# The order of a two-layer trunk's instructions, searched for from twelve beginnings instead of one

## The chip, the cores and the metric

The kernel runs on one core of one Trainium2 chip. Its time is the device time of one execution in microseconds (us). Before the change it took 1188.26 us, the median of three runs (1187.7 to 1189.58).

## The reference

The model has two layers over 512 tokens of width 1024, in float32. Cut to what matters, a layer is:

```python
h   = rms_norm(x, g_pre_mix)
u_pool, q, k, v, iq, ik, iw = split(h @ w_in)        # 512 | 512 | 512 | 512 | 512 | 64 | 8 columns
q, k, iq, ik = rope on the first 16 of 64 columns of each head
a   = pool_mixer(u_pool)         # 4 groups of 128 channels: mean over the last 2, 4, 8 or 16 tokens
                                 # less the token itself, then a 128x128 matmul and a scale
score = sum over 8 heads of iw * relu(iq . ik / 8)   # keys of later 64-token chunks left out
b   = attention of 8 heads over the 128 keys with the highest score of each query
x   = x + rms_norm(concat(a, b) @ w_out, g_post_mix)
f   = relu(rms_norm(x, g_pre_ffn) @ w_ff1) ** 2 @ w_ff2      # width 4096
x   = x + rms_norm(f, g_post_ffn)
```

## The kernel before

**Arithmetic.** Every float32 factor is split into a high part, rounded to the matmul's format, and the remainder, and a product is three matmuls (`mm3`: high x high, high x low, low x high). The weights come from HBM through `WeightStream`: raw loads of 512 KB into two buffers (`wraw`), and two more for the MLP's first matrix (`uraw`). Each chunk of 128 rows is then split into one of eight `ws` tiles, the high part by a copy that may run on VectorE (DVE) or ScalarE (ACT), the low part by a subtraction on DVE. All but one block of the MLP's first product are done by a scheme with seven half-sized products in place of eight (`unit_products`, tiles `one` and `two`), which needs sums of weight quarters on DVE.

**Stages of a layer.** The token norm and transposes (`pre_norm`, tiles `h`, `hT`, `A`), the indexer's product and scores (`pi`, `lg`, `sc`), q, k and v (`rows_block`, tiles `pg`), meanwhile the selection of keys on DVE (`select`: 15 or 16 rounds of eight maxima and their replacement, tiles `m` and `bias`), attention for four blocks of 128 queries (`s`, `pt`, `pT`, `po`) beside the pooling mixer (`pool`, `mx`, `dh`, `mix`), the output projection (`out_pair`, `pg`), the two norms (`post_norm`, `pre_norm`; their reciprocal root `rstd` runs on GpSimd, POOL), and the MLP: four groups of two blocks of the first product and two halves of the second, summed in `facc`.

**What sets the order.** The program isn't issued as it is written. Every call on an engine goes through `_Recorder` (its call, line 372, is where the profile places nearly all instructions), which notes the operation, its planned cost (`cost`), what it reads and writes, and, for operations given to `either`, the two engines that could run it. Nothing moves between engines otherwise. `Planner.issue` (line 193) then chooses one order for all engines: it ranks the operations by the longest way to the end, adds a noise that a seed draws, and calls `sweep` (line 246). A sweep is a simulation of the engines: it takes the operations in time, on each engine the ready one with the smallest key, with planned costs and planned delays between engines (`LATENCY`, `DMA_STARTS`, `DMA_LANDS`), a slowing of DVE beside POOL (`shared`) and the choice between two engines (`sooner`, which from the second sweep on looks at latest times too). A second sweep backward gives each operation a latest time, from which come the keys of the next forward sweep. Of all forward sweeps the one with the shortest planned span is issued, in the order of its start times; the engines then run their instructions in that order and wait for each other by semaphores. Weight loads keep their written order among each other. The search runs on the host while the program is built and is no part of the time.

Of the kernel before, what the change touches and what calls it, by code (L numbers as in the profile page):

```python
# [82 lines left out]
class Planner:  # L83
# [11 lines left out]
    AGAIN = 100.0  # L95
    SPARE = 20000.0
    RELOAD = 54.0
    SWEEPS = 40
    SEED = 53
    NOISE = 500.0  # L100
    SLOWED = 0.35
# [91 lines left out]
    def issue(self):  # L193

        ops = self.ops
        n = len(ops)
        succ = [[] for _ in range(n)]
        pred = [[] for _ in range(n)]  # L200
        for i, (_, deps, soft) in enumerate(ops):
            for group, hard in ((deps, True), (soft, False)):
                for d in group:
                    succ[d].append((i, hard))
                    pred[i].append((d, hard))
        rank = [0.0] * n
        for i in range(n - 1, -1, -1):
            e, cost = ops[i][0][0][:2]
            tail = 0.0
            for j, hard in succ[i]:  # L210
                tail = max(tail, rank[j] + (self.lag(e, ops[j][0][0][0]) if hard else -cost))
            rank[i] = cost + tail
        state, key, late, best = self.SEED, [], None, None
        for r in rank:
            state = (state * 1103515245 + 12345) % 2 ** 31
            key.append(self.NOISE * (state / 2.0 ** 31 - 0.5) - r)
        for _ in range(self.SWEEPS):
            start, end, way = self.sweep(key, pred, succ, late)
            span = max(end)
            if best is None or span < best[0]:  # L220
                best = (span, start, way)
            back, _, _ = self.sweep([-t for t in end], succ, pred, None, way)
            late = [span - b for b in back]
            key = [late[i] - ops[i][0][way[i]][1] for i in range(n)]
        self.planned, start, way = best
        for i in sorted(range(n), key=lambda i: (start[i], i)):
            ops[i][0][way[i]][2]()

# [1049 lines left out]
```

## Time and profile before

| what | value |
|---|---|
| median of three runs | 1188.26 us (1187.7 to 1189.58) |
| the profiled execution's own time | 1189.19 us |
| its span, first to last instruction | 1187.4 us |
| mean granted TensorE clock | 0.992 |
| TensorE (PE) matmuls | 1154.9 us busy, 6888 instructions |
| weight loads of PE (PEld) | 1008.9 us busy |
| DVE | 962.8 us busy, 2134 instructions |
| ACT | 593.5 us busy, 1279 instructions |
| POOL | 31.5 us busy, 79 instructions |
| read from HBM | 112.27 MB |

An engine's busy time is the union of its instructions' times; what is left of a stretch is idle. PEclk is the share of TensorE's full clock that was granted. The chain of waits is followed back from the last instruction, at each step to what released it or to the instruction ahead of it on its engine.

### The profile page before, as it was taken

The page shows a single profiled execution, that of the slowest core. Times are in us where ns is not written, and L with a number is a line of the kernel's source. Part 1 is how long each engine was busy: PE and PEld are TensorE (multiplying, and loading weights), DVE is VectorE, ACT ScalarE, POOL GpSimd, SP SyncE. Part 2 cuts the span into 40 slices and gives each one's busy share as a digit, 9 for nine tenths or more (in the row PEclk, how much of TensorE's full clock was granted, in tenths as well). Part 3 has the DMA queues.
Part 4 walks back from the last instruction along what each step waited for, and adds up shares of the span by engine and source line. Part 5 has one row for each costly group of instructions (what it writes and reads, how often), then busy time and mean ns, then how long its engine had stood idle before and what let it go on. Part 6 is the DMA issues. An engine that isn't in the chain of part 4 may idle for free.

```text
span 1187.4 us, 18436 instructions
## 1 busy us (share of the span) xinstructions
PE 1154.9 (97%) x6888; PEld 1008.9 (85%) x6888; DVE 962.8 (81%) x2134; ACT 593.5 (50%) x1279; POOL 31.5 (3%) x79
## 2 busy tenths in 40 slices
PE   6999999999999999999999999899999999999997
PEld 6988888789899898899898888777998998988985
DVE  7799999889569579577698999998994785875965
ACT  7545796687226036035275277876760440430621
POOL 2000000010000000000010000001000000000001
PEclk9999998999999999999999999999999999999999
DMA  7221222451423223223233121134542241251231
GB/s 249 71 72 36 71 72 72 142 184 66 161 74 132 95 72 132 82 71 97 60 112 89 54 72 54 54 115 134 160 141 73 71 161 54 72 177 36 72 107 71
DMA packets 62169, 115.55 MB, mean 97 GB/s; under 512 B 5248, under 2 KB 10368, under 8 KB 62080
## 3 DMA queue, kind: packets, MB, share of 16 engines
q1 hardware_dynamic: 62080, 114.38, 30.2%
q8 instruction: 54, 0.88, 0.3%
q14 instruction: 35, 0.29, 0.1%
HBM read 112.27 MB, written 2.10 MB: 96 GB/s over the span
## 4 chain that ended last, share of the span: by engine, by line
PE 61%; DVE 26%; DMA 5%; ACT 4%; issue 3%; POOL 1%; SPq 0%; DVEq 0%; ACTq 0%; POOLq 0%
PE pg L372 33%; PE one L372 9%; PE two L372 7%; DVE ws L372 6%; DVE bias L372 3%; PE pi L372 3%; PE pf L372 3%; DVE m L372 3%; DMA wraw<-in_w_out_dram 2%; DMA uraw<-in_w_ff_dram 2%; DVE mx L372 1%; PE lg L372 1%; DVE s L372 1%; PE po L372 1%; DVE pT L372 1%
## 5 line engine op out<-in xcount | busy, mean ns | idle before, releaser
L372 PE MATMUL pg<-ws,f 128*128 128x512 f32 x768 | 230.5, 394 | 0.0
L372 PE MATMUL pg<-ws,A 128*128 128x512 f32 x864 | 227.5, 401 | 0.9 <-DVE A L372 0.6
L372 ACT ACTIVATE ws<-wraw 128x512 fp32r<-128x512 f32 (+1 forms) x182 | 112.9, 632 | 183.8 <-PE pg L372 127.3
L372 DVE TENSOR_TENSOR ws<-wraw,ws 128x512 fp32r<-128x512 f32 (+1 forms) x288 | 194.4, 689 | 5.9 <-ACT ws L372 3.8
L372 PEld LDWEIGHTS pg<-ws,A 128*128 128x128 f32 x864 | 157.7, 188 | 34.3 <-DVE pn L372 1.6
L372 PE MATMUL pg<-ws,f1h 128*128 128x512 f32 x512 | 167.2, 394 | 0.5 <-ACT fr L372 0.5
L372 PEld LDWEIGHTS pg<-ws,f 128*128 128x128 f32 x768 | 141.1, 188 | 29.0
L372 PEld LDWEIGHTS pg<-ws,f1h 128*128 128x128 f32 x512 | 95.6, 188 | 22.3 <-ACT fr L372 1.0
L372 DVE TENSOR_TENSOR ws<-uraw,ws 128x512 fp32r<-128x512 f32 x168 | 111.7, 686 | 2.0 <-ACT ws L372 0.7
L372 DVE CAST ws<-wraw 128x512 fp32r<-128x512 f32 (+1 forms) x106 | 45.0, 426 | 75.2 <-PE pg L372 64.3
L372 PE MATMUL two<-A,ws 128*128 128x256 f32 x672 | 104.9, 281 | 0.0
L372 PE MATMUL pg<-ws,f1l 128*128 128x512 f32 x256 | 95.8, 393 | 0.0
L372 PEld LDWEIGHTS two<-A,ws 128*128 128x128 f32 x672 | 92.3, 188 | 1.9
L372 ACT ACTIVATE ws<-uraw 128x512 fp32r<-128x512 f32 x95 | 57.7, 627 | 67.8 <-PE pg L372 29.7
L372 ACT ACTIVATE s<-s,st 128x384 f32<-128x384 f32 (+3 forms) x118 | 64.7, 565 | 21.4 <-DVE st L372 20.8
L372 ACT ACTIVATE fr<-fr 128x512 f32<-128x512 f32 (+1 forms) x109 | 63.5, 596 | 21.0 <-DVE fr L372 20.1
L372 DVE TENSOR_TENSOR facc<-pg,facc 128x512 f32<-128x512 f32 x48 | 32.7, 688 | 46.2 <-PE pg L372 46.2
L372 DVE CAST ws<-uraw 128x512 fp32r<-128x512 f32 x73 | 30.4, 424 | 41.7 <-PE pg L372 32.6
L372 PE MATMUL pi<-ws,A 128*128 128x292 f32 x384 | 61.8, 310 | 1.1 <-DVE ws L372 0.8
L372 PE MATMUL pool<-A,ws 128*128 128x512 f32 x192 | 59.2, 405 | 0.0
L372 PEld LDWEIGHTS pg<-ws,f1l 128*128 128x128 f32 x256 | 48.0, 188 | 10.9
L372 PE MATMUL one<-A,ws 128*128 128x256 f32 x336 | 57.0, 280 | 0.0
(189 smaller groups left out, 2203.5 us busy)
## 6 DMA issues: line engine op xcount, KB each, us to landing
wraw<-in_w_ff_dram SPq DMA_DIRECT2D x72, 512.0 KB, 3.8
uraw<-in_w_ff_dram SPq DMA_DIRECT2D x56, 512.0 KB, 4.9
wraw<-in_w_out_dram SPq DMA_DIRECT2D x32, 512.0 KB, 3.7
wraw<-in_w_in_dram SPq DMA_DIRECT2D x24, 512.0 KB, 3.6
wraw<-in_w_in_dram SPq DMA_DIRECT2D x8, 584.0 KB, 4.3
wraw<-in_w_in_dram SPq DMA_DIRECT2D x16, 256.0 KB, 2.9
x<-in_x_dram SPq DMA_DIRECT2D x4, 512.0 KB, 6.5
out_dram<-x SPq DMA_DIRECT2D x8, 256.0 KB, 2.1
```

The source lines that it names most:

```text
L372: lambda: getattr(self.real, method)(*args, **kw), self.port(method, out, reads))
```

## The change

Before, the search is one series of 40 sweeps from one set of keys. After it, there are twelve series of 16 sweeps. The first begins with the same keys. Each later one begins with new keys: for every operation half of the sum of its start in the best order so far and of the key that the backward sweep made of that order, and a noise that is four times as wide. The latest times are forgotten at each beginning. The best order over all series is issued. The operations, their tiles and their costs are the same.

```diff
--- before.py
+++ after.py
@@ -95,7 +95,8 @@
     AGAIN = 100.0
     SPARE = 20000.0
     RELOAD = 54.0
-    SWEEPS = 40
+    SWEEPS = 16
+    BEGINNINGS = 12
     SEED = 53
     NOISE = 500.0
     SLOWED = 0.35
@@ -210,19 +211,22 @@
             for j, hard in succ[i]:
                 tail = max(tail, rank[j] + (self.lag(e, ops[j][0][0][0]) if hard else -cost))
             rank[i] = cost + tail
-        state, key, late, best = self.SEED, [], None, None
-        for r in rank:
-            state = (state * 1103515245 + 12345) % 2 ** 31
-            key.append(self.NOISE * (state / 2.0 ** 31 - 0.5) - r)
-        for _ in range(self.SWEEPS):
-            start, end, way = self.sweep(key, pred, succ, late)
-            span = max(end)
-            if best is None or span < best[0]:
-                best = (span, start, way)
-            back, _, _ = self.sweep([-t for t in end], succ, pred, None, way)
-            late = [span - b for b in back]
-            key = [late[i] - ops[i][0][way[i]][1] for i in range(n)]
-        self.planned, start, way = best
+        state, best = self.SEED, None
+        for begin in range(self.BEGINNINGS):
+            key, late = [], None
+            for i in range(n):
+                state = (state * 1103515245 + 12345) % 2 ** 31
+                mine = -rank[i] if begin == 0 else best[1][i] + best[3][i]
+                key.append(self.NOISE * (1 + 3 * (begin > 0)) * (state / 2.0 ** 31 - 0.5) + mine)
+            for _ in range(self.SWEEPS):
+                start, end, way = self.sweep(key, pred, succ, late)
+                span = max(end)
+                back, _, _ = self.sweep([-t for t in end], succ, pred, None, way)
+                late = [span - b for b in back]
+                key = [late[i] - ops[i][0][way[i]][1] for i in range(n)]
+                if best is None or span < best[0]:
+                    best = (span, start, way, [0.5 * (k - t) for k, t in zip(key, start)])
+        self.planned, start, way, _ = best
         for i in sorted(range(n), key=lambda i: (start[i], i)):
             ops[i][0][way[i]][2]()
 
```

## Rows read from the trace of the kernel before

**Rows 1.** The page: busy time by engine, and the chain's shares by engine.
```profile
PE 1154.9 (97%) x6888; PEld 1008.9 (85%) x6888; DVE 962.8 (81%) x2134; ACT 593.5 (50%) x1279; POOL 31.5 (3%) x79
...
PE 61%; DVE 26%; DMA 5%; ACT 4%; issue 3%; POOL 1%; SPq 0%; DVEq 0%; ACTq 0%; POOLq 0%
```

**Rows 2.** Windows by stage: stretch, length, engines' busy time (instructions), PEclk, DMA share, GB/s.
```profile
0.00:28.00 28.00, 18.54 (x114) 17.28 (x114) 20.53 (x59) 20.21 (x44) 6.56 (x36) 1.00 0.80 264
28.00:111.00 83.00, 82.56 (x466) 70.91 (x467) 73.81 (x197) 41.81 (x91) 0.80 (x4) 1.00 0.20 58
111.00:172.00 61.00, 60.91 (x338) 51.20 (x337) 60.64 (x166) 50.22 (x112) 0.23 (x2) 1.00 0.24 70
172.00:192.00 20.00, 18.32 (x91) 15.25 (x90) 18.95 (x64) 13.69 (x38) 0.11 (x1) 0.74 0.15 51
192.00:249.00 57.00, 56.14 (x291) 44.85 (x289) 51.77 (x149) 42.54 (x118) 3.36 (x5) 1.00 0.45 137
249.00:297.00 48.00, 45.84 (x376) 44.75 (x377) 45.75 (x78) 35.66 (x77) 4.06 (x3) 1.00 0.34 115
297.00:598.00 301.00, 298.77 (x1785) 263.86 (x1784) 212.97 (x373) 101.99 (x186) 2.08 (x4) 1.00 0.30 98
598.00:634.00 36.00, 34.95 (x273) 34.19 (x271) 30.80 (x73) 24.44 (x63) 3.84 (x7) 1.00 0.28 86
634.00:697.00 63.00, 62.71 (x311) 51.18 (x309) 59.72 (x159) 29.91 (x56) 0.29 (x2) 1.00 0.25 72
697.00:760.00 63.00, 62.95 (x350) 53.01 (x349) 62.76 (x172) 50.61 (x113) 0.35 (x3) 1.00 0.23 74
760.00:772.00 12.00, 8.78 (x46) 6.84 (x46) 11.29 (x40) 7.78 (x21) 0.00 (x0) 0.86 0.01 2
772.00:834.00 62.00, 60.39 (x314) 47.50 (x314) 57.80 (x169) 41.98 (x120) 4.52 (x5) 1.00 0.42 128
834.00:881.00 47.00, 46.64 (x383) 45.39 (x382) 46.10 (x79) 38.43 (x81) 1.97 (x3) 1.00 0.40 128
881.00:1179.00 298.00, 297.37 (x1774) 262.69 (x1772) 204.84 (x361) 92.98 (x168) 1.38 (x2) 1.00 0.29 93
1179.00:1187.40 8.40, 0.00 (x0) 0.00 (x0) 5.06 (x10) 1.26 (x4) 2.00 (x2) 0.66 0.36 135
```

**Rows 3.** Waits of PE: who waited for whom, us in total, times, longest.
```profile
PE hT L372 <- ACT h L372: 9.7, 3, 8.1
```

**Rows 4.** Windows around the two falls of the granted clock.
```profile
176.00:180.00 4.00, 2.93 (x17) 2.45 (x17) 3.96 (x14) 3.90 (x9) 0.00 (x0) 0.77 0.00 0
...
176.00:188.00 12.00, 10.62 (x44) 8.82 (x44) 10.95 (x36) 8.11 (x22) 0.00 (x0) 0.59 0.00 0
764.00:768.00 4.00, 2.94 (x14) 2.94 (x15) 3.94 (x16) 1.51 (x4) 0.00 (x0) 0.65 0.00 0
```

**Rows 5.** A window inside the first layer's MLP.
```profile
300.00:325.00 25.00, 25.00 (x109) 20.22 (x108) 13.61 (x24) 4.18 (x7) 0.00 (x0) 1.00 0.46 153
```

**Rows 6.** The chain in order of time: start, us, what.
```profile
1.17 4.89 DMA gain<-in_g_pre_mix_dram
...
169.84 0.60 DVE ws L372
...
182.11 0.43 PE mix L372
...
233.96 3.61 DMA wraw<-in_w_out_dram
...
297.17 37.12 PE pg L372 x160
```

**Rows 7.** Groups of instructions: out<-in, shape, count | busy us, mean ns | idle before, releaser.
```profile
L372 ACT ACTIVATE ws<-wraw 128x512 fp32r<-128x512 f32 (+1 forms) x182 | 112.9, 632 | 183.8 <-PE pg L372 127.3 <-DMA wraw<-in_w_ff_dram 28.3 <-DMA wraw<-in_w_out_dram 13.3
L372 DVE CAST ws<-wraw 128x512 fp32r<-128x512 f32 (+1 forms) x106 | 45.0, 426 | 75.2 <-PE pg L372 64.3 <-DMA wraw<-in_w_ff_dram 5.3 <-DMA wraw<-in_w_out_dram 2.9
L372 POOL TENSOR_TENSOR rstd<-rstd,neg_half 128x1 f32<-128x1 f32 x32 | 27.8, 874 | 570.1 <-DVE rstd L372 564.8 <-ACT f1h L372 5.3
```

## The prediction

> **What bounds the kernel now.** The first view is the page's list of busy shares with the chain of waits below it [rows 1]. The reader sees TensorE (PE) busy for 1154.9 of 1187.4 us and holding 61% of the chain, VectorE (DVE) busy for 962.8 us and holding 26%. So PE sets the time and DVE is the engine that it waits for. The second view cuts the span into stages [rows 2]: in each row the stretch less PE's busy time is PE idle, and PEclk is the clock that PE was granted. The idle time is 32.53 us in all: 9.46 in the first 28 us, where nothing can be multiplied before the first norm (one wait of 8.1 us on ACT [rows 3], behind the gain vector that lands after 4.89 us [rows 6]); 8.40 behind the last product; and 14.67 in the thirteen rows between. That 14.67 us, and what the clock takes beside it, is what another order of the same instructions can work on.
>
> Where it lies: 1.68 us in 172:192 and 3.22 in 760:772, where both layers leave the selection and attention stretch, in which DVE is busy for 60.64 of 61 us and 62.76 of 63 [rows 2]. There PE has used up the big products that it laid between the attention pieces and runs at DVE's pace. The rest lies at the hand-over from the output projection to the MLP (2.16 and 0.36 us), in the projection itself (0.86 and 1.61), in the MLP (2.23 and 0.63) and at the start of each layer (0.44, and 1.05 + 0.29).
>
> The clock belongs to the first of these. In 176:180 PE was busy for 2.93 of 4 us and the mean grant falls to 0.77; over 176:188 it is 0.59, over 764:768 it is 0.65 [rows 4]. The level that these means mix with full speed is 1.2 of 2.4 GHz: a 512-column product that takes 0.232 us in the MLP (37.12 us for 160) takes 0.43 us there [rows 6]. PE's busy time in the two stretches, 10.62 and 2.94 us, would have been 10.62 x 0.59 = 6.27 and 2.94 x 0.65 = 1.91 at full clock, so the clock cost 4.35 and 1.03 us. The room for an order is therefore 14.67 + 4.35 + 1.03 = 20.05 us, 1.7% of the span.
>
> **The change part by part.** It adds and removes no computation, load or tile: the list of recorded operations is the same, and issue() alone differs.
>
> First, the search. The first beginning draws the same noise from the same seed on the same ranks, so its 16 sweeps are the first 16 of the 40 before; sweeps 17 to 40 are gone. Eleven more beginnings start from half the sum of the best order's start times and of its backward keys, with noise of up to 1000 ns either way instead of 250, 16 sweeps each, and the shortest planned order of all 192 is issued. Cost on the chip: none, it is host work. Its planned span can be longer than before only if the winner of before lay in the dropped sweeps and all eleven later beginnings miss it.
>
> Second, how far a planned gain reaches the chip. I compare the planner's constants with single rows. PE: 4.5 + 512/2.25 = 232 ns against 232 [rows 6]. DVE: 70 + 1.04 x 512 = 602 ns for a product or difference against 600 on the chain. A 512 KB load: 1170 to start, 1456 to move and 1050 to land, 3.68 us, against 3.61. These agree within some 2%, so most of a planned gain should be seen. What the plan has wrong or not at all: the 32 reciprocal roots on POOL, 874 ns against 520 planned [rows 7], and the fall of the clock.
>
> Third, copies that may go to either engine. A split copy takes 426 ns on DVE and 632 on ACT [rows 7]. A different choice moves some of these. In the stretches where DVE is full (60.64 of 61) a copy moved to ACT frees 0.43 us of DVE, in the MLP (DVE 212.97 of 301 us) it is worth nothing, since PE covers it there; if that cover went, PE would wait up to 0.63 us for each copy. I take this within the sum below and not beside it.
>
> Fourth, loads. They stay in their written order on SP's queue, 512 KB at a time with two raw buffers, so a split that is planned earlier or later moves the load behind it. The chain passes through such loads in the output projection (3.61 us) [rows 6]; as PE idles for only 0.86 and 1.61 us there, I take nothing for it, with 1.61 us as the most it can give and the same as the most it can cost.
>
> **The sum.** How much of the 20.05 us a longer search finds is not in a trace of before, so I bound it and choose by the nearest rows. The lower end is a loss, priced under the rivals; the upper end is the whole 20.05 us. The nearest rows are the two layers, which do the same work and which one search ordered differently. If both had the better of the two orders, each stage would save the difference [rows 2, 4]: selection with attention 0.09 - 0.05 = 0.04; the stall behind it (1.68 + 4.35) - (3.22 + 1.03) = 1.78; output projection 1.61 - 0.86 = 0.75; hand-over 2.16 - 0.36 = 1.80; MLP 2.23 - 0.63 = 1.60. Sum 5.97 us. I take two thirds, 4.0 us, as some of that better order in one layer was bought with a worse neighbour (the layer with the quiet hand-over has the dearer projection). The head I take as 0 (the gain vector and the norm come first in any order) and the tail as 0: its 8.40 us hold 5.06 us of DVE work, so 3.34 us is the most it could give. Against the profiled execution: span 1187.4 - 4.0 = 1183.4, and with the 1.8 us around it (1189.19 - 1187.4) 1185.2. That execution lies 0.93 us above the median of the three runs, 1188.26, so on the scale of the median I forecast 1184.3 us.
>
> **One rule against these rows.** In 300:325 PE is busy for all 25 us, product behind product, while its weight loads are busy for 20.22, 81% [rows 5]; over the span they are at 85% [rows 1]. So 85% here is a full PE, not a PE with 15% to spare. The Trainium skill (Perfetto Trace Analysis, Identifying the Most-Contended Engine) says that matmul busy time is a poor gauge of the headroom and that the busy share of LDWEIGHTS is a good one. By it, as an estimate, the room would be 15% of 1187.4 = 178 us instead of 20, and the same fifth of it would be a saving of 36 us; this trace does not agree.
>
> **The rivals.**
> *No change that can be measured (1187.5 us).* The order is shorter on paper, but what it shortens are waits that are not as planned. For it: POOL's roots run 0.35 us over plan, and each norm's chain (root, scaling, transposes) is on the chain of waits; 8 tiles of the two hand-overs alone make 2.8 us that the plan does not see, which leaves 4.0 - 2.8 = 1.2. Rounded down for the loads, 0.8. Against it: PE and DVE, 87% of the chain, run as planned.
> *Slower (1192.3 us).* One more stall of the kind at 172:192, for instance at a hand-over where PE already idles for 2.16 us. The planner has no term for the clock, so laying the big products earlier costs it nothing, and PE runs dry before DVE is through. Price: idle and clock as in the first layer, 1.68 + 4.35 = 6.03 us; with half of the forecast's gain, 2.0, it makes +4.0. It decides as soon as one such stretch is added and the rest gains less than 3.6 us (6.03 less 2.4). The trace has two such stretches where the search was free to avoid them, which speaks for it; no hand-over of before has a lowered clock, which speaks against. The Trainium skill (TensorE: Matmul & The Clock Gate, HAM oscillation) also has gaps in PE's work bring the clock down; here the fall stands beside PE's idle time in both places.
> *Much faster (1178 us).* The search finds half of the room, 10 us: both stalls shortened until the clock holds (5.4 us), and a third of the 14.67 us of idle time. For it: eleven beginnings that each keep the best so far; against: PE is already busy for 98.7% of the time between head and tail.
> *The longer search finds nothing (1188.3 us).* The noise is too coarse and the best order is one of the first sweeps, much like that of before. Nothing in the trace bears on it.
>
> **How the numbers follow.** Forecast 0.44, no measurable change 0.24, slower 0.17, much faster 0.12, nothing found 0.02, the saving of 36 us by the weight loads' share 0.01. About 0.2%, 2.4 us, is what can be told from no change. Faster: 0.44 + 0.12 + 0.01 = 0.57; within: 0.24 + 0.02 = 0.26; slower: 0.17. The range reaches from just past the much faster case, 1177, to just short of the slower case with no other gain than is forecast for it, 1191.5, and leaves out some 0.15. The forecast's own range is 1181 to 1185.8.
>
> **What would show it.** Right: the same count of matmuls (6888) and of loads; PE idle between head and tail at 10 to 12 us instead of 14.67, most of the drop in the stalls behind attention and at the first hand-over; fewer than 13 us at the lower clock; selection and attention with DVE still full, so that no time is saved inside them. Wrong: PE idle unchanged or moved to another place; a third stretch with a grant near 0.5; or a gain that lies in the head or the tail, which I took as fixed.

## The result, and the profile after

The changed kernel takes 1181.97 us (median of 4 runs, 1181.6 to 1183.65) against 1188.74 us for the kernel before in the same comparison: a ratio of 0.9946, 95% interval 0.9929 to 0.9963. That is 6.8 us faster; 4.0 us were forecast (1184.3 us, range 1177 to 1191.5). The profiled execution fell from 1189.19 to 1181.99 us, its span from 1187.4 to 1180.2.

The page's shares first, which answer to [rows 1]: PE is busy for as many instructions and 3.4 us less, DVE does the same work, and the chain of waits has more PE and less DVE in it.

```profile
PE 1151.5 (98%) x6888; PEld 1004.9 (85%) x6888; DVE 963.3 (82%) x2139; ACT 594.6 (50%) x1274; POOL 29.6 (3%) x79
...
PE 65%; DVE 21%; ACT 7%; DMA 5%; issue 2%; POOL 0%; SPq 0%; DVEq 0%; ACTq 0%; POOLq 0%
```

Now the stages, cut at about the same places of the program as in [rows 2] and with the same columns:

```profile
0.00:28.00 28.00, 19.04 (x117) 18.39 (x117) 20.77 (x61) 16.94 (x38) 5.00 (x36) 1.00 0.78 252
28.00:111.00 83.00, 82.57 (x465) 70.81 (x463) 75.83 (x202) 42.52 (x88) 0.60 (x4) 1.00 0.21 62
111.00:172.00 61.00, 60.92 (x342) 51.12 (x341) 60.70 (x168) 51.74 (x113) 0.24 (x2) 1.00 0.26 79
172.00:190.00 18.00, 16.27 (x93) 12.28 (x92) 17.81 (x58) 11.86 (x32) 0.11 (x1) 1.00 0.06 16
190.00:245.00 55.00, 53.71 (x282) 42.19 (x281) 51.74 (x152) 42.09 (x116) 3.41 (x4) 1.00 0.45 138
245.00:294.00 49.00, 48.11 (x390) 46.74 (x389) 47.47 (x82) 39.15 (x81) 2.83 (x4) 1.00 0.42 136
294.00:592.00 298.00, 297.54 (x1779) 262.95 (x1778) 214.11 (x378) 97.78 (x180) 2.83 (x5) 1.00 0.30 98
592.00:628.00 36.00, 36.00 (x278) 35.49 (x278) 30.91 (x74) 24.70 (x63) 4.60 (x7) 1.00 0.26 80
628.00:690.00 62.00, 61.08 (x303) 49.81 (x301) 57.94 (x156) 29.48 (x56) 0.29 (x2) 1.00 0.24 69
690.00:753.00 63.00, 62.20 (x345) 51.77 (x344) 62.43 (x170) 51.62 (x115) 0.35 (x3) 1.00 0.25 76
753.00:765.00 12.00, 10.11 (x59) 8.35 (x58) 11.07 (x39) 9.75 (x25) 0.00 (x0) 0.86 0.01 2
765.00:826.00 61.00, 59.49 (x310) 46.86 (x309) 56.29 (x164) 43.08 (x121) 4.32 (x5) 1.00 0.42 130
826.00:876.00 50.00, 49.02 (x389) 47.02 (x388) 48.46 (x84) 38.49 (x80) 2.16 (x4) 1.00 0.40 118
876.00:1172.00 296.00, 295.43 (x1766) 261.13 (x1764) 202.76 (x355) 93.98 (x169) 1.38 (x2) 1.00 0.29 95
1172.00:1180.20 8.20, 0.00 (x0) 0.00 (x0) 4.96 (x10) 1.45 (x4) 1.44 (x2) 0.64 0.34 128
```

Stretch less PE's busy time, row by row: PE's idle time between head and tail went from 14.67 to 11.55 us. It fell in the first layer's hand-over to the MLP (2.16 to 0.89) and MLP (2.23 to 0.46), at the start of the second layer (1.05 to 0.00) and in its stall behind attention (3.22 to 1.89). It rose in the second layer's q and k products (0.29 to 0.92), selection and attention (0.05 to 0.80) and hand-over (0.36 to 0.98), and in the first layer's projection (0.86 to 1.29). In the first layer's stall it stayed (1.68 to 1.73). With the head (9.46 to 8.96) and the tail (8.40 to 8.20) idle time gives 3.8 of the span's 7.2 us.

The rest of the 7.2 us is 3.4 us of shorter busy time, with as many instructions, and the clock is of that size. The windows around the two stalls, as in [rows 4]:

```profile
176.00:180.00 4.00, 2.85 (x21) 2.33 (x20) 3.91 (x11) 2.86 (x6) 0.00 (x0) 1.00 0.00 2
180.00:184.00 4.00, 3.42 (x20) 2.40 (x19) 3.97 (x16) 2.74 (x8) 0.00 (x0) 1.00 0.00 0
...
758.00:762.00 4.00, 2.42 (x11) 1.93 (x11) 4.00 (x20) 3.43 (x12) 0.00 (x0) 0.91 0.03 6
762.00:766.00 4.00, 4.00 (x16) 3.29 (x16) 3.10 (x11) 1.78 (x6) 0.00 (x0) 0.66 0.00 0
```

In the first layer PE is as idle at 176:180 as before (2.85 us busy against 2.93) and the grant stays at 1.00, where it was 0.77 and then lower. In the second it falls as before. By the same working as in the prediction the clock now costs 2.42 x 0.09 + 4.00 x 0.34 = 1.6 us against 5.4: 3.8 us, in this pair of executions. The 3.8 is PE's time at the lower clock, not yet the kernel's: DVE was busy for 10.95 of the 12 us there [rows 4], so PE might have waited for part of it at full clock too. What the clock is worth in the whole time is taken up with run 1.

### The profile page after: what moved, and what is told of

Its sections match the earlier page's. It is cut to its first block, busy times and chain, and to the rows that moved or that the text cites. A ratio compares the mean times of both kernels' runs of the same rounds, so it can differ in the third digit from the quotient of the medians.

```text
span 1180.2 us, 18409 instructions
## 1 busy us (share of the span) xinstructions
PE 1151.5 (98%) x6888; PEld 1004.9 (85%) x6888; DVE 963.3 (82%) x2139; ACT 594.6 (50%) x1274; POOL 29.6 (3%) x79
## 4 chain that ended last, share of the span: by engine, by line
PE 65%; DVE 21%; ACT 7%; DMA 5%; issue 2%; POOL 0%; SPq 0%; DVEq 0%; ACTq 0%; POOLq 0%
PE pg L376 35%; PE one L376 11%; PE two L376 8%; DVE ws L376 5%; PE pi L376 5%; DVE bias L376 3%; DVE m L376 3%; PE pf L376 2%; PE lg L376 2%; ACT s L376 1%; DMA uraw<-in_w_ff_dram 1%; DVE pT L376 1%; DMA wraw<-in_w_ff_dram 1%; DMA wraw<-in_w_out_dram 1%; DVE mx L376 1%
## 5 line engine op out<-in xcount | busy, mean ns | idle before, releaser
L376 PE MATMUL pg<-ws,A 128*128 128x512 f32 x864 | 230.8, 403 | 1.3 <-DVE pn L376 1.2
L376 PE MATMUL pg<-ws,f 128*128 128x512 f32 x768 | 224.2, 394 | 0.3 <-DVE f L376 0.3
L376 ACT ACTIVATE ws<-wraw 128x512 fp32r<-128x512 f32 (+1 forms) x175 | 108.1, 631 | 175.0 <-PE pg L376 132.9
L376 PE MATMUL two<-A,ws 128*128 128x256 f32 x672 | 113.6, 281 | 0.0
L376 DVE CAST ws<-wraw 128x512 fp32r<-128x512 f32 (+1 forms) x113 | 47.9, 426 | 67.4 <-PE pg L376 56.1
L376 PEld LDWEIGHTS two<-A,ws 128*128 128x128 f32 x672 | 96.1, 188 | 2.1 <-ACT p L376 0.2
L376 ACT ACTIVATE fr<-fr 128x512 f32<-128x512 f32 (+1 forms) x112 | 66.4, 598 | 23.6 <-DVE fr L376 22.2
L376 ACT ACTIVATE s<-s,st 128x512 f32<-128x512 f32 (+3 forms) x116 | 63.8, 565 | 20.3 <-DVE st L376 19.8
L376 PEld LDWEIGHTS pi<-ws,A 128*128 128x128 f32 x384 | 55.9, 196 | 2.1 <-DVE A L376 1.3
```

The lines of the kernel that those rows point to most:

```text
L376: lambda: getattr(self.real, method)(*args, **kw), self.port(method, out, reads))
```

## The experiments

Two theories were tried. By "plan", a shorter planned order means shorter waits everywhere and a shorter time. By "clock", most of the gain is the first layer's stretch at half clock that is gone. A third joined them: an order's time may differ from another's by chance, whatever the plan. Each kernel was timed beside the kernel before, whose medians in the four comparisons were 1189.1, 1189.15, 1189.02 and 1187.9 us.

**1. Fill the gap ahead of the clock's fall.** The order of before; behind the three mix products of one pooling group in the first layer the same three are issued again.

```diff
             ops[i][0][way[i]][2]()
+            for j in self.again.get(i, ()):
+                ops[j][0][way[j]][2]()
...
                 mm3(ps, lambda a: wp[a][:, g], lambda b: dh[:, b], True, True)
+                if l == 0 and g == 0:
+                    planner.again[len(planner.ops) - 1] = range(first, len(planner.ops))
```

> The order of before, with the three 512-column products of one pooling group of the first layer (the mix matmuls at 174.4 to 176.1 us) issued a second time, right behind themselves. They write the same sums again, so the result is the same; they add 3 x 0.232 = 0.70 us of work to PE just where PE idled 0.83 us ahead of the fall of the clock. Theory 'clock' (most of the change's gain is the first layer's 10 us at half clock that are gone): if the fill is enough, the granted clock stays at 1.00 over 176:188, the 4.35 us come back and the time is 1188.7 - 4.35 + 0 to 0.7 = 1184.4 to 1185.1. Theory 'plan' (the gain is shorter waits throughout, the clock beside the point): nothing gained, 1188.7 to 1189.4. If the clock falls all the same, the run only prices the fill and tells nothing.

Measured: 1187.19 us, ratio 0.9989 (0.9981 to 0.9998). Three useless products made the kernel no slower, rather 0.1% faster. In the execution that was traced the clock was not kept. Its windows:

```profile
176.00:180.00 4.00, 3.49 (x25) 2.64 (x23) 3.96 (x15) 3.89 (x9) 0.00 (x0) 1.00 0.01 2
180.00:184.00 4.00, 3.19 (x21) 2.40 (x19) 4.00 (x19) 2.97 (x12) 0.00 (x0) 1.00 0.00 0
184.00:188.00 4.00, 3.62 (x13) 2.72 (x13) 3.95 (x11) 2.04 (x8) 0.00 (x0) 0.53 0.02 4
188.00:192.00 4.00, 4.00 (x19) 3.58 (x18) 3.37 (x12) 0.96 (x5) 0.00 (x0) 0.61 0.44 131
```

PE's idle time at 176:180 halved, and the fall moved from 176:188 to 184:192. That execution has the lowest mean grant of the eleven, 0.992; their median is 0.995, against 0.9935 for the 26 of before beside them, so the clock may have held in some of the others, and no trace shows it. The run can't give the full price of the clock. The runs of before can: 86 executions of one and the same program, with a mean granted clock between 0.990 and 0.997. The 20 at 0.992 or less have a median of 1189.26 us, the 11 at 0.996 or more 1186.88. So the clock varies with the order unchanged, and it is worth some 2.4 us from end to end. (As an estimate from [rows 2], the first layer's fall, 0.26 of 20 us, is 0.0044 of the span's mean grant, about what separates the two groups.) The four runs of after were at 0.995 or 0.996. Against those 11 runs after is 1186.88 - 1181.97 = 4.9 us faster: by this working that part is not the clock, and at most 1.9 of the 6.8 us is. Theory "clock" falls as the main cause of the whole gain.

**2. Five beginnings.** `BEGINNINGS = 5`.

> The change with 5 beginnings instead of 12: the first five of the same twelve, so its plan cannot be shorter than after's nor longer than before's. Theory 'plan': a time between the two, about half the gain, 1185.3 (1183.5 to 1187), and PE idle between head and tail between 11.6 and 14.7 us. Theory 'clock': the time goes by whether the first layer's clock falls: 1186.5 to 1188.7 with the fall, 1182 to 1184 without.

Measured: 1188.63 us, ratio 0.9998 (0.9987 to 1.0010), at a median grant of 0.997: a shorter plan and a good clock, and no gain. Both theories fail here. In the second layer's MLP this order waits for a load, by the chain of waits (start, us, what) and by DVE's timeline (start, us, instruction, in brackets the idle time before it and what ended it):

```profile
1040.84 7.17 DMA uraw<-in_w_ff_dram
```

```profile
1048.11 0.69 DVE L376 TENSOR_TENSOR usum<-uraw 128x512 f32<-128x512 f32 x1 [2.18 <-DMA uraw<-in_w_ff_dram]
```

The load took 7.2 us and DVE stood for 2.18 us of it. PE lost 0.97 us by it, of 17.47 us that it idles between head and tail in this trace, more than before's 14.67 and outside the 11.6 to 14.7 that "plan" expected. So this wait is one among many:

```profile
28.00:1179.80 1151.80, 1134.33 (x6774) 987.77 (x6772) 941.44 (x2077) 568.18 (x1221) 26.37 (x41) 1.00 0.29 93
```

**3. Twelve independent beginnings.**

```diff
-                mine = -rank[i] if begin == 0 else best[1][i] + best[3][i]
-                key.append(self.NOISE * (1 + 3 * (begin > 0)) * (state / 2.0 ** 31 - 0.5) + mine)
+                mine = -rank[i]
+                key.append(self.NOISE * (state / 2.0 ** 31 - 0.5) + mine)
```

> Twelve beginnings of 16 sweeps, but none from the best order so far: each draws its own noise of 250 ns either way on the ranks, as the first does. Theory 'plan, and beginning from the best order matters': about half of the gain, 1185.3 (1183.5 to 1187). Rival 'the number of tries alone': all of it, 1182. Theory 'clock': as in the run with five beginnings, by the first layer's granted clock.

Measured: 1184.39 us, ratio 0.9965 (0.9952 to 0.9977): about two thirds of the gain without beginning from the best order, within the range that "plan" gave and short of the whole gain of the rival.

**4. 24 beginnings, with less noise.** `BEGINNINGS = 24`, and the later noise times 1.2 in place of 4.

> A longer search: 24 beginnings, and the later ones with noise 1.2 times the first's instead of 4 times. Its plan is shorter than after's. Theory 'plan': faster than after, 1179.5 to 1181. Theory 'clock': no faster than after when its clock is as after's, 1181 to 1183; slower, up to 1187, when a second stretch at half clock comes.

Measured: 1176.62 us (1176.17 to 1176.99), ratio 0.9902 (0.9890 to 0.9915). It beats both kernels, by more than "plan" expected; "clock" allowed no gain over after. The stretch between head and tail, here 28:1166.8 (before: 1151 us long with 14.67 us idle), has 10.06 us of PE idle time:

```profile
28.00:1166.80 1138.80, 1128.74 (x6767) 986.09 (x6765) 937.20 (x2071) 569.10 (x1225) 24.24 (x41) 1.00 0.30 94
```

PE is also busy for less time, 1147.2 us over the span against 1154.9: of the two stalls only the second shows a lower grant.

```profile
172.00:188.00 16.00, 14.13 (x87) 11.54 (x86) 15.69 (x55) 12.24 (x34) 0.03 (x1) 1.00 0.11 34
...
756.00:764.00 8.00, 6.60 (x32) 5.61 (x33) 7.91 (x30) 6.24 (x19) 0.00 (x0) 0.79 0.01 2
```

**5 and 6. One layer in each order.** Both orders are kept, cut at the operation where the program begins the second layer, the parts aligned by their mean start near the cut, and issued by start as soon as all predecessors are. The order of before is its search's 14th sweep, so it is also the best of after's first beginning, from which these runs take it.

```diff
+        at = [head[1][i] if i < cut else tail[1][i] + shift for i in range(n)]
+        way = [(head if i < cut else tail)[2][i] for i in range(n)]
...
```

> The first layer in the order of after and the second in the order of before, merged at the operation with which the second layer is begun in the program. Reading of the two traces: the last product of the first layer's MLP ends 5.8 us sooner in after (592.2 against 598.0 us), the span 7.2. Theory 'the gain lies in the first layer, and stays when the second is ordered as before': 1188.9 - 5.8 = 1183.1 (1182 to 1184.5), with the clock at 1.00 over 176:188. Rival 'an order works only as a whole, a splice loses it': 1186 or more, with new idle time of PE around 590 to 640 us.

> The other half: the first layer in the order of before and the second in that of after. Theory 'the gain lies in the first layer': 1188.9 - 1.4 = 1187.5 (1186.5 to 1188.5), with the first layer's fall of the clock as in before. Rival 'as a whole': no gain or slower, 1189 or more.

Measured: the first layer alone 1184.47 us, ratio 0.9964 (0.9952 to 0.9975); the second alone 1188.04 us, 0.9992 (0.9983 to 1.0001). The gain lies in the first layer, 4.3 us by its ratio; 0.36 and 0.08% together are 0.44% of the whole 0.54%, which the intervals hold. The clock went with the first layer's order: the trace with after's first layer has a grant of 1.00 in its stall, the one with before's 0.79 in 176:192. The splice is not free: PE idles 1.95 us around it, by the window of the run with the first layer alone (1.05 us in the same window before).

```profile
592.00:640.00 48.00, 46.05 (x328) 43.47 (x328) 40.87 (x93) 31.98 (x81) 4.71 (x7) 1.00 0.32 100
```

**7 and 8. Another seed.** `SEED = 54` in the changed kernel, and the same with one beginning.

> The change with another seed, 54 for 53, so that all twelve beginnings draw other noise. Its plan is shorter than before's and a little longer than after's. Theory 'plan': faster than before by most of the change's gain, 1183 to 1186. Theory 'luck of one order' (any order lies within some 4 us of another, whatever its plan): anything from 1183 to 1193, no nearer to after than to before.

> The same other seed with the first beginning alone, so the search of before with another draw. Its plan is longer than before's. Theory 'plan': slower than before, 1190 to 1195. Theory 'luck of one order': no nearer to slower than to faster. By both the difference between this run and the one with twelve beginnings of the same seed is the change's worth at this seed.

Measured: twelve beginnings 1187.67 us, ratio 0.9986 (0.9976 to 0.9996); one beginning 1193.16 us, 1.0035 (1.0023 to 1.0047). The longer plan is slower, as "plan" said, and at this seed the change is worth 0.9986 / 1.0035 = 0.9951, as at the first (0.9946). But the order with twelve beginnings comes out 0.4% above after, slower than "plan" allowed. The clock has a part in the slow one: its mean grants are 0.989 to 0.993, and its trace has a lower grant at four places, of which no other trace has 104:116 and 608:612.

```profile
104.00:116.00 12.00, 10.44 (x50) 8.65 (x50) 11.92 (x32) 8.76 (x16) 0.00 (x0) 0.72 0.31 89
184.00:188.00 4.00, 3.77 (x21) 3.78 (x21) 3.97 (x18) 2.50 (x9) 0.00 (x0) 0.60 0.00 0
608.00:612.00 4.00, 4.00 (x21) 4.00 (x20) 3.00 (x5) 2.07 (x6) 0.00 (x0) 0.57 0.87 273
768.00:776.00 8.00, 6.59 (x30) 6.01 (x31) 7.18 (x26) 4.09 (x12) 0.00 (x0) 0.57 0.23 69
```

**9. The first layer up to its MLP alone.** As in 5, with the cut where the first MLP begins.

> The first layer up to its MLP in the order of after, all that follows in the order of before. Reading of the two traces: at the last half-sized product of the first MLP block after is 2.7 us ahead (293.8 against 296.5 us), and it gains as much again in the MLP that follows. Theory 'mixing stage': 1189.1 - 2.7 = 1186.4 (1185.4 to 1187.4), and the other 1.6 us of the run with the whole first layer belong to the MLP. Rival 'the stall and its clock are all of the first layer's gain': 1184.5, as that run.

Measured: 1185.32 us, ratio 0.9973 (0.9962 to 0.9984), 3.2 us, between the two expectations. Most of the first layer's gain lies ahead of its MLP; the MLP's part, 0.9973 to 0.9964, is not told apart from nothing. Ahead of the MLP it is hardly idle time: in 28:294 PE idles 4.98 us, in 28:297 of before 5.23. What differs is the first stall's grant.

```profile
28.00:294.00 266.00, 261.02 (x1559) 222.34 (x1558) 253.13 (x658) 185.08 (x427) 7.16 (x15) 1.00 0.29 90
172.00:190.00 18.00, 16.26 (x93) 12.27 (x92) 17.81 (x58) 11.99 (x32) 0.11 (x1) 1.00 0.05 14
```

So of this part of the gain the clock is the likely cause, with some 2.9 of the 3.2 us by this one trace. That is more than the 1.9 us that the medians allowed the clock; the interval of the 3.2 us, 1.9 to 4.5, holds both, and no run settles the share.

**10. 24 beginnings with the change's own noise.** `BEGINNINGS = 24`.

> 24 beginnings with the change's own noise, 4 times the first's: the change's twelve and twelve more, so its plan is no longer than after's. It parts the two changes of the run with 24 closer beginnings (1176.6 us). Theory 'closeness of the beginnings': 1181 to 1182.5, as after. Rival 'the number of beginnings': 1177 to 1179.

Measured: 1187.84 us, ratio 0.9993 (0.9985 to 1.0002). This search contains after's, and its plan is no longer; the chip takes 0.47% more, and both theories of this run fall. A shorter plan by itself does not make a shorter time. One place where it lost is plain in the trace, in the first layer's MLP. The chain of waits there, and then the timeline of SP's queue, DVE and PE:

```profile
292.90 5.91 DMA wraw<-in_w_ff_dram
```

```profile
292.90 0.37 SPq L376 DMA_DIRECT2D wraw<-in_w_ff_dram  x1
293.32 0.47 SPq L376 DMA_DIRECT2D uraw<-in_w_ff_dram  x1
295.01 0.37 SPq L376 DMA_DIRECT2D wraw<-in_w_ff_dram  x1
295.48 1.33 SPq L376 DMA_DIRECT2D uraw<-in_w_ff_dram  x2
...
298.84 0.43 DVE L376 CAST ws<-wraw 128x512 fp32r<-128x512 f32 x1 [2.05 <-DMA wraw<-in_w_ff_dram]
299.18 0.42 DVE L376 CAST f<-fr 128x512 fp32r<-128x512 f32 x1
...
299.66 0.50 PE L376 MATMUL pg<-ws,f 128*128 128x512 f32 x1 [1.36 <-DVE f L376]
```

Four more loads are issued behind the one at 292.90 before it lands, after 5.9 us, where [rows 6] had 3.61 for one of this size. DVE stands for 2.05 us at the split of that load; behind the split in its order stands the MLP's own copy to `f`, for which PE waits, though ACT had written the copy's input by 296.92.

**11. The planner's costs nearer to the rows.** As 4, with POOL's root at 860 ns and loads landing 950 ns later.

> 24 closer beginnings, and two costs of the planner nearer to the rows: the reciprocal root on POOL 860 ns for 520 (rows: 874 and 815 ns), a load lands 950 ns later than planned before (rows: medians of 4.9 us for the loads that come in pairs, up to 7.2). Theory 'what the plan misjudges is paid on the chip': faster than the run with 24 closer beginnings, 1173 to 1176, with less idle time of PE at the hand-overs. Rival 'those costs hardly matter, the draw does': 1176.5 to 1182, either side of that run and no faster.

Measured: 1185.51 us, ratio 0.9970 (0.9959 to 0.9982): 0.7% slower than run 4, so that expectation fell, and the rival's range was passed too. PE's idle time in the MLP did go (0.27 us in 593):

```profile
296.00:594.00 298.00, 297.73 (x1786) 263.85 (x1784) 216.03 (x381) 99.56 (x183) 3.24 (x5) 1.00 0.31 100
880.00:1175.00 295.00, 295.00 (x1768) 261.57 (x1767) 205.14 (x360) 92.28 (x166) 1.44 (x2) 1.00 0.29 94
```

But the hand-overs took more than that back, 3.25 us in 807:880 alone, where run 4 has 0.73 in 800:870. Both lines, run 11 first:

```profile
807.00:880.00 73.00, 69.75 (x488) 63.82 (x487) 67.53 (x121) 52.67 (x113) 7.38 (x7) 1.00 0.42 129
```

```profile
800.00:870.00 70.00, 69.27 (x483) 62.98 (x482) 67.10 (x120) 52.16 (x113) 6.06 (x7) 1.00 0.43 137
```

**12. The late load's split behind what PE needs.** The order of run 10 with three instructions moved (the numbers are the operations' places in the program as written).

```diff
+        for moved, behind in (((2780, 2781), 2801), ((2794,), 2831)):
+            order = [i for i in order if i not in moved]
+            k = order.index(behind) + 1
+            order[k:k] = moved
...
```

> The order of the run with 24 far beginnings with three instructions moved and nothing else: in the first layer's MLP, the split of the weight load that landed 5.91 us after its issue (DVE waited 2.05 us for it at 296.8 us, ACT 1.98 us) stands behind the MLP's own copy and difference on DVE (tile f) and behind the first relu on ACT, not ahead of them. In the run before PE idled 1.36 us at 298.3 to 299.7 us for that difference. Theory 'a load later than planned holds up the queue behind it': the idle time of 1.36 us goes, the end of that MLP group comes 1.4 to 2.5 us sooner after the same start, the time falls from 1187.8 to 1186.4 (1185.3 to 1187). Rival 'another wait takes its place': PE waits as long for the split itself a little later, 1187.8 (1187.2 to 1188.5).

Measured: 1186.76 us, ratio 0.9993 (0.9983 to 1.0004), the same ratio as run 10: the times don't tell the two apart. The profile does, at that place (the load in the chain of waits, then the timeline of DVE and PE):

```profile
291.46 5.31 DMA wraw<-in_w_ff_dram
```

```profile
295.51 0.43 DVE L383 CAST f<-fr 128x512 fp32r<-128x512 f32 x1 [0.16 <-ACT fr L383]
295.97 0.69 DVE L383 TENSOR_TENSOR f<-fr,f 128x512 fp32r<-128x512 f32 x1
296.80 0.43 DVE L383 CAST ws<-wraw 128x512 fp32r<-128x512 f32 x1
...
297.28 0.50 PE L383 MATMUL pg<-ws,f 128*128 128x512 f32 x1 [0.43 <-DVE ws L383]
```

The copy to `f` no longer waits for the load. PE's wait is 0.43 us in place of 1.36, and it is now for the split itself: the rival, at a third of its price. Not all of the difference is the move's: the load landed after 5.31 us here and 5.91 in run 10, 0.60 us sooner. From its landing to PE's next product it is 0.51 us here (296.77 to 297.28) and 0.85 there (298.81 to 299.66), so the move itself is worth some 0.34 us. So the mechanism is shown where it happens, at about a quarter of the 1.36 us; the rest is the load and its split themselves. Its worth in the whole time stays below what these comparisons resolve.

## Why the prediction was right, and where it was not

**What bounds the kernel.** Right. In the profiles the gain is PE's idle time between head and tail (14.67 to 11.55 us, 10 to 12 forecast) and the clock (1.6 us lost against 5.4). Head and tail, taken as 0, gave 0.5 and 0.2 us. DVE stayed full in selection and attention (60.70 of 61 us, 62.43 of 63), as forecast, and no time was saved there.

**How far a planned gain reaches the chip.** This step, "most of a planned gain should be seen", is the weak one. The forecast did not use the plan itself, though each planner works out its planned span (`planned`) on the host, before anything runs on the chip. For the kernels that one search with the planner's own costs gave:

| order | planned us | measured us |
|---|---|---|
| seed 54, one beginning | 1157.6 | 1193.16 |
| before | 1153.7 | 1188.74 |
| five beginnings | 1150.9 | 1188.63 |
| independent | 1150.2 | 1184.39 |
| seed 54, twelve | 1148.7 | 1187.67 |
| after | 1147.6 | 1181.97 |
| 24 far | 1147.5 | 1187.84 |
| 24 closer | 1145.9 | 1176.62 |

After's plan is 6.1 us shorter than before's, and 6.8 were measured. The trend is the plan's, but what the chip takes beyond the plan runs from 30.8 us (24 closer) to 40.3 (24 far), so that after and 24 far, next to each other in it, came out 5.9 us the wrong way round. The sign held at both seeds: each gained 0.5% over one beginning (of 40 sweeps at the first seed, of 16 at the other). The size was not; with the draw of run 10 the same kind of search would have come out as "no change that can be measured". That this order's gain lay within the range is in part luck.

**The sum.** Forecast 4.0 us, measured 6.8. By its terms, before to after in the profiles: the hand-overs gave 0.65 us (1.27 in the first layer less 0.62 in the second) and the MLPs 1.83, where the better of the two layers had promised 1.80 and 1.60. The projection, 0.75 promised, gave -0.33 over both layers. Selection with attention lost 0.74 us, and the q and k products ahead of it 0.63 in the second layer, where the prediction had no change. The stall was mis-sized: 1.78 forecast, 1.28 of idle time and 3.8 of clock measured. The clock's price was taken from one execution; over the 86 runs of before it moves from run to run. By these runs up to 1.9 us of the medians' difference is its share, by run 9 some 2.9; either is less than the 3.8 of the profiles. So the sum came near the measured time by terms that were off both ways.

**The clock's rule.** After idles as much at 176:180 as before and keeps the clock, so idle time beside the fall, which is all that the two places of [rows 4] showed, does not say when it comes. The order has a say in it all the same: the three traces with before's first layer (before, runs 1 and 6) have a fall in its stall, the three with after's (after, runs 5 and 9) have none. The Trainium skill (TensorE: Matmul & The Clock Gate, HAM oscillation) lets gaps in PE's work bring the clock down; the second layer here agrees (2.42 of 4 us busy, then 0.66), the first does not.

**Loads.** Costed at nothing, with 1.61 us either way. The prediction checked the plan's 3.68 us against one load of 3.61; the 56 `uraw` loads of before had a median of 4.9, in its own list of DMA issues:

```profile
uraw<-in_w_ff_dram SPq DMA_DIRECT2D x56, 512.0 KB, 4.9
```

Runs 10 and 12 show the cost: a load that lands after 5.9 us holds DVE for 2.05 us and PE for 1.36, of which the order of DVE's queue made some 0.34. The windows of the two loads, before's of 3.61 us and run 10's of 5.91, have the 16 DMA engines busy for 0.45 and 0.82 of the time:

```profile
233.96:237.57 3.61, 3.61 (x17) 2.94 (x16) 2.81 (x5) 0.64 (x1) 0.00 (x0) 1.00 0.45 145
```

```profile
292.90:298.81 5.91, 5.39 (x35) 4.50 (x33) 3.89 (x7) 1.40 (x3) 0.00 (x0) 1.00 0.82 265
```

The Trainium skill (DMA: Bandwidth & Descriptors, Issuing engines are not separate DMA queues) says that transfers started by different engines run on the same 16 DMA engines and interleave. The trace of run 10 agrees as far as it goes, with five loads issued between 292.90 and 296.81 and the first of them late; all five start on SP's queue, so loads from another engine are not shown.

**The rivals.** "Slower" did not come for after: no third stretch at a lower clock. Its mechanism exists, as run 8 shows, with two added stretches and 1193.16 us. "Much faster" is what run 4 reached. "Nothing found" is excluded, since beginnings beyond the first changed the order and the time. The 36 us by the weight loads' share did not come: they are busy for 85% of the span before and after, with 6.8 us between the two.

**What stays open.** Why orders with almost the same plan differ by up to 6 us. Late loads are one cause, shown at one place; falls of the clock are another, seen in run 8; the stalls behind attention and the hand-overs, where PE idles in every trace, differ from order to order as well, and no run took them apart. How the gain divides between the clock and shorter waits is known only within the bounds above. That 24 closer beginnings do better because they are closer is not shown either: it is one draw at one seed.

## What to carry to other kernels

A longer search over instruction orders is a gain that must be measured order by order: its plan decides on average, and a single order lies a few tenths of a per cent to either side. Read the plan's own gain before forecasting, then compare several orders on the chip and keep the fastest. In an in-order queue, put what the bound engine waits for ahead of anything that waits for a load.

## What the runs showed of the hardware

One program, run 86 times, had a mean granted clock between 0.990 and 0.997, and its time moved with it by some 2.4 us. Three added products of 0.70 us in a gap of PE made the kernel no slower, and in the two traced executions the fall of the clock stood at 176:188 without them and at 184:192 with them. A 512 KB load took 3.6 us at a DMA share of 0.45 and 5.9, with four more issued behind it, at 0.82.
